# Meta-token states in two row groups, a written order of additions, and a residual added in PSUM, in a hybrid decoder layer

## The chip, the cores and the metric

The kernel runs on one core of one Trainium2 chip. The time is device microseconds of one execution; the number given is the median over several runs. A core has TensorE (PE in the profile; its weight loads are listed apart as PEld), VectorE (DVE), ScalarE (ACT), GpSimd (POOL) and SyncE (SP, which only issues transfers here). Products go into PSUM, which has eight banks of 512 fp32 columns; the other engines take them from there.

## The reference

One decoder layer on 512 tokens of width 1024, with 16 learned meta tokens put ahead of them (528 positions):

- `u = rmsnorm(h)`, and `proj = u @ w_in`, which is cut into the inputs of two branches and two sigmoid gates.
- The pooling branch takes causal means over windows of 2, 4, 8 and 16 positions, subtracts the input, and goes through a grouped matrix and `w_pool_up`.
- The state-space branch (SSD) has 8 groups of 4 heads with 64 channels. Tokens are worked on in chunks of 128; the 16 meta tokens are a chunk of their own, the first. Each chunk gives a state `sum over its tokens of B * (decay * dt * x)`, 128 x 64 for each head; states are carried on from chunk to chunk, `st[c+1] = decay_c * st[c] + (state of chunk c)`, and read out with C. So the meta chunk's product is `st[0]`: a contraction over only 16 positions, 128 x 256 for a group's four heads.
- `h = h + (gate_pool * y_pool + gate_ssd * y_ssd) @ w_o`, then `h = h + relu(rmsnorm(h) @ w_ff1)^2 @ w_ff2`, and a last rmsnorm with the weight `final_norm_w`. The 16 meta rows are dropped.

All is in fp32. Only the results of the 512 tokens are returned.

## The kernel before

**Precision.** Most products are made of halves: an fp32 number x is split into `hi`, x rounded to the type fp32r by a ScalarE copy, and `lo = x - hi`, by a VectorE subtraction. A product then takes three matmuls, hi x hi, hi x lo, lo x hi. A product of plain fp32 operands, as in the SSD part, is carried out as two passes, each with its own weight load and its own row in the trace.

**Stages.** Weights come in blocks of 128 x 1024 in a fixed order: SyncE's queue loads a block into one of three `raw` buffers (L85, L107), ScalarE writes `whi` (L93), VectorE `wlo` (L94), with four buffers of each. In order of time there are: the norm and the first projections; eight SSD groups, each woven by generators with the projections of the next group (`weave`); the `psp` products; the pooling stage with the `psl` products; the merge with `w_o`; the MLP in products over halves and sums of halves (Strassen's scheme in Winograd's form), and the last chunk of the MLP straight into the output.

**A group of the SSD** (`ssd`). TensorE transposes three chunks of B (`ptb`, L474) and B's 16 meta columns (L475), the meta columns of the two x tiles (`ptm`, L480), and the x tiles (`ptx`, L488). ScalarE takes B out (`btok`, `btm`, L476 and L477), VectorE multiplies x by dt (`xdtm`, L481; `xdt`, L489) and by the decay (`xddm`, L494; `xdd`, L495). Then come C x B (`pcb`, L522) and the states (`pst`): the meta product (L529), with 16 rows of `btm` as weights and 256 columns of `xddm`, and three products of full chunks (L531), two products to a bank. ScalarE copies `st[0]` out (L533), VectorE carries the states on (L538, L539), and `po` (L550) and `py` (L556) are the outputs. `dtm` and `decm` hold dt and decay of the meta positions, 16 partitions with all 32 heads beside each other; `dt_out` (L374 to L387) makes them by transposes and a small product.

**The `psl` stage.** The last two of the 16 rows of y are multiplied into `psl` (8 products, in four PSUM buffers), and each is added onto `acc[d]` by VectorE (L897). After it in the program come the blocks `wgb` and the last pool gate (`pgp`), the grouped matrix (`pg`), and `pool_pair`, which takes two raw blocks `a1` and `a2`, forms sums of their halves in `sm` (L818, L819) and splits them (`whiA`, `whiS`, `whiD`, `whiB`) for products with u.

**The end.** For each of four row tiles t and two column halves, products go into PSUM (L1491), VectorE adds them onto `ht`, which holds the residual (L1494), ScalarE sums the squares (L1368), VectorE multiplies by `fw` (L1498). `finish` makes the reciprocal root (L1376 to L1380) and scales the row tile on both engines (L1381, L1383). The last half of the last row tile is done in two parts of 256 columns.

**What sets the order.** Each engine works through a queue in a fixed order. That order isn't the program's: a planner fills it ahead of time from the program's order, the dependences and its own estimates of durations, and an instruction later in the program goes ahead where the earlier one would wait. `with tc.issue_after(i)` holds what is issued under it behind instruction i on the same engine. Before the change, L818 is held behind `psl_split`, the last subtraction of a weight split ahead of `wgb`.

Of the kernel before, what the change touches and what calls it, by code (L numbers as in the profile page):

```python
# [14 lines left out]
P = 128  # L15
D = 1024
SEQ = 512
NM = 16
# [45 lines left out]
def kernel(ctx: ExitStack, tc, xT, x, w, f1, f2, vec, fnw, out):  # L64
# [22 lines left out]
    def block_part(t, c):  # L87
        block_load(t, c)
        block_split(t, c)

    def block_split(t, c):
        b, raw, hi, lo = t
        act.copy(hi[:, c], raw[:, c])  # L93
        split_end[0] = dve.tensor_tensor(lo[:, c], raw[:, c], hi[:, c].bitcast(F32), op=ALU.subtract)  # L94

    split_end = [None]

    def block():
        t = block_tiles()
        block_part(t, slice(0, 1024))  # L100
        return t[2:]
# [52 lines left out]
    dtm = const.tile([NM, 2, HEADS], F32, name="dtm")  # L154
    dec = const.tile([P, 4, HEADS], F32, name="dec")
    cdec = const.tile([P, 4, HEADS], F32, name="cdec")
    decm = const.tile([NM, HEADS], F32, name="decm")
# [183 lines left out]

    v, e, s, s2, pl, dt, acs = (dtile(n) for n in ("dv", "de", "ds", "ds2", "dpl", "ddt", "dacs"))
# [27 lines left out]
    def dt_out():  # L370

        pt = psum1("pt_dt")
        for j, src in enumerate((dt, acs)):
            pe.transpose(pt[:, j * P : (j + 1) * P], src[:, :P], ident)  # L374
            pe.transpose(pt[:NM, 256 + j * H : 256 + (j + 1) * H], src[:H, P:], ident[:H, :H])
        dve.tensor_copy(dtok.rearrange("p a c h -> p (a c h)"), pt[:, :256])
        dve.tensor_copy(dtm.rearrange("p a h -> p (a h)"), pt[:NM, 256 : 256 + 2 * H])
# [3 lines left out]
        pe.matmul(pq[:NM, 128 : 128 + H], sel[:NM, 1, :NM], dtm[:, 1, :], start=True, stop=True)  # L381
        fl = lambda t: t.rearrange("p c h -> p (c h)")
        dve.tensor_tensor(fl(dec), pq[:, :128], fl(dtok[:, 1, :, :]), op=ALU.subtract)
        dve.tensor_tensor(decm, pq[:NM, 128 : 128 + H], dtm[:, 1, :], op=ALU.subtract)
# [73 lines left out]
    def ssd(g, cur):  # L458
# [10 lines left out]
        xdtm = gs.tile([NM, R, 64], F32, tag="xdtm", name=f"xdtm{g}")  # L469
        btok = gs.tile([P, 3, P], F32, tag="btok", name=f"btok{g}")  # L470
        btm = gs.tile([NM, P], F32, tag="btm", name=f"btm{g}")
# [3 lines left out]
        pe.transpose(ptb[:NM, 3 * P :], bt[:, :NM], ident)  # L475
        act.copy(btok.rearrange("p c n -> p (c n)"), ptb[:, : 3 * P])  # L476
        b_meta[g] = act.copy(btm, ptb[:NM, 3 * P :])  # L477
        pm = psum1(f"ptm{g}")
        for i in range(2):
            pe.transpose(pm[:NM, i * P : (i + 1) * P], xc[:, i, :NM], ident)  # L480
        dve.tensor_tensor(xdtm, pm[:NM, :256].rearrange("p (r d) -> p r d", r=R),  # L481
                          bc(dtm[:, 0, hs], 64), op=ALU.mult)
# [10 lines left out]
        xddm = gs.tile([NM, R, 64], F32, tag="xddm", name=f"xddm{g}")  # L493
        dve.tensor_tensor(xddm, xdtm, bc(decm[:, hs], 64), op=ALU.mult)  # L494
# [33 lines left out]
        pv = [pss[c // 2][:, (c % 2) * 256 : (c % 2) * 256 + 256] for c in range(4)]  # L528
        pe.matmul(pv[0], btm, flat(xddm), start=True, stop=True)  # L529
        for c in range(3):  # L530
# [1109 lines left out]
```

## Time and profile before

| | us |
|---|---|
| median of 3 runs | 1003.55 (1003.0 to 1003.87) |
| profiled execution, its own time | 1003.78 |
| its span in the trace | 1002.1 |
| TensorE busy | 993.4 |
| VectorE busy | 793.0 |
| ScalarE busy | 602.2 |
| GpSimd busy | 88.1 |

The granted TensorE clock was 0.998 in the profiled execution. A row of the trace in order of time begins with the start and the duration in us, then engine, line, operation, what is written and read, shapes and count; brackets at its end give how long the engine was idle ahead of it and what released it. Matmuls overlap their neighbours, so a sum of durations is more than the time that they take: the step from one start to the next is what counts. A row with x8 covers from the first start to the last end.

### The profile page before, as it was taken

How to read it: one execution, taken by the hardware profiler on the slowest of the kernel's cores; microseconds unless marked ns; L12 is line 12 of the kernel's file. 1: busy time of each engine (PE TensorE's matmuls, PEld its weight loads, DVE VectorE, ACT ScalarE, POOL GpSimd, SP SyncE). 2: the span in 40 equal slices, each digit the busy share in tenths (PEclk: the TensorE clock that was granted, in tenths of full speed). 3: DMA queues.
4: the chain of work that ended last, by engine and by line, in shares of the span. 5: the costliest groups of instructions: out<-in, count | busy, mean ns of one | idle time of the engine just before them, and what ended most of it. 6: DMA issues, size and time to landing. Idle time of an engine off the chain costs nothing.

```text
span 1002.1 us, 15532 instructions
## 1 busy us (share of the span) xinstructions
PE 993.4 (99%) x6093; PEld 877.8 (88%) x6093; DVE 793.0 (79%) x1147; ACT 602.2 (60%) x838; POOL 88.1 (9%) x148
## 2 busy tenths in 40 slices
PE   9999999999999999999999999999999999999997
PEld 7889898999889998988898888888889999999986
DVE  7988797979736687978789567877988888878885
ACT  8675958585827339483255343377666656656654
POOL 0022101111002011002210001121100000000000
PEclk9999999999999999999999999999999999999999
DMA  7278753677238635407987632779764454464432
GB/s 248 89 284 227 221 159 117 200 181 235 64 103 258 162 106 149 143 27 223 293 190 226 227 105 72 227 175 321 187 195 148 149 188 148 147 191 146 126 105 85
DMA packets 56202, 171.47 MB, mean 171 GB/s; under 512 B 6400, under 2 KB 7744, under 8 KB 55104
## 3 DMA queue, kind: packets, MB, share of 16 engines
q1 hardware_dynamic: 36576, 105.86, 32.4%
q0 software_dynamic: 18832, 63.71, 24.2%
q8 instruction: 48, 0.79, 0.3%
q10 hardware_dynamic: 720, 0.91, 0.3%
q14 instruction: 26, 0.21, 0.1%
HBM read 161.90 MB, written 48.40 MB: 210 GB/s over the span
## 4 chain that ended last, share of the span: by engine, by line
PE 97%; DMA 1%; DVE 1%; ACT 0%; issue 0%; SPq 0%; ACTq 0%; DVEq 0%
PE px L191 12%; PE px L1288 8%; PE alpha L1356 6%; PE pz L191 6%; PE px L193 6%; PE px L1291 4%; PE alpha L1359 3%; PE pgp L191 3%; PE pz L193 3%; PE pgs L191 3%; PE py L556 2%; PE pso L127 2%; PE po L550 2%; PE pso L128 1%; PE wo_alpha L1050 1%; PE pgp L193 1%
## 5 line engine op out<-in xcount | busy, mean ns | idle before, releaser
L93 ACT CAST whi<-raw 128x1024 fp32r<-128x1024 f32 (+2 forms) x98 | 98.6, 1015 | 105.3 <-PE px L193 30.9
L94 DVE TENSOR_TENSOR wlo<-raw,whi 128x1024 fp32r<-128x1024 f32 (+2 forms) x98 | 114.6, 1176 | 55.4 <-ACT whi L93 33.9
L191 PE MATMUL px<-uh,whi 128*128 128x264 f32 (+1 forms) x448 | 113.2, 291 | 0.0
L193 PE MATMUL px<-ul,whi 128*128 128x264 f32 (+1 forms) x448 | 110.5, 285 | 0.0
L191 PEld LDWEIGHTS px<-uh,whi 128*128 128x128 f32 x448 | 84.6, 189 | 1.8 <-issue 1.4
L193 PEld LDWEIGHTS px<-ul,whi 128*128 128x128 f32 x448 | 84.2, 188 | 0.4 <-issue 0.2
L1063 DVE TENSOR_TENSOR ht<-ht,alpha 128x1024 f32<-128x1024 f32 x35 | 42.7, 1219 | 29.5 <-PE alpha L1356 29.5
L986 ACT CAST shi<-rawf 128x1024 fp32r<-128x1024 f32 x42 | 44.2, 1052 | 28.8 <-PE alpha L1359 18.3
L191 PE MATMUL px<-uh,wlo 128*128 128x264 f32 (+1 forms) x448 | 58.5, 283 | 0.0
L191 PEld LDWEIGHTS px<-uh,wlo 128*128 128x128 f32 x448 | 55.9, 188 | 0.0
L1356 PE MATMUL alpha<-shi,hh 128*128 128x512 f32 x140 | 55.2, 394 | 0.0
L1359 PE MATMUL alpha<-shi,hl 128*128 128x512 f32 x140 | 54.7, 391 | 0.0
L987 DVE TENSOR_TENSOR slo<-rawf,shi 128x1024 fp32r<-128x1024 f32 x42 | 51.1, 1218 | 0.6 <-ACT shi L986 0.6
L1291 PE MATMUL px<-vsl,shi 128*128 128x256 f32 x192 | 47.4, 280 | 0.0
L1288 PE MATMUL px<-vsh,shi 128*128 128x256 f32 x192 | 47.4, 281 | 0.0
L193 PE MATMUL pz<-ul,whi 128*128 128x512 f32 x112 | 43.6, 389 | 0.0
L191 PE MATMUL pz<-uh,whi 128*128 128x512 f32 x112 | 43.6, 389 | 0.0
L577 DVE RECIPROCAL rs<-rs 128x128 f32<-128x128 f32 x32 | 27.2, 908 | 13.9 <-ACT rs L575 13.8
L1356 PE MATMUL alpha<-slo,hh 128*128 128x512 f32 x140 | 37.4, 389 | 0.0
L1288 PEld LDWEIGHTS px<-vsh,shi 128*128 128x128 f32 x192 | 36.2, 188 | 0.9
L1291 PEld LDWEIGHTS px<-vsl,shi 128*128 128x128 f32 x192 | 36.1, 188 | 0.9
L1291 PE MATMUL px<-vl,shi 128*128 128x256 f32 x144 | 36.1, 283 | 0.0
(550 smaller groups left out, 2857.0 us busy)
## 6 DMA issues: line engine op xcount, KB each, us to landing
raw<-in_w SPq DMA_DIRECT2D x104, 512.0 KB, 4.5
f_t<-in_f POOLq DMA_DIRECT2D x38, 512.0 KB, 6.8
f_s<-in_f POOLq DMA_DIRECT2D x26, 512.0 KB, 8.7
b<-in_f SPq DMA_DIRECT2D x21, 512.0 KB, 4.7
rawf<-in_f SPq DMA_DIRECT2D x36, 256.0 KB, 3.2
rawf<-f_t SPq DMA_DIRECT2D x36, 256.0 KB, 2.9
abc<-acs_d POOLq DMA_DIRECT2D x8, 1024.0 KB, 7.5
f_t<-f_t POOLq DMA_DIRECT2D x12, 512.0 KB, 4.3
```

Of the source, the lines that this page charges most:

```text
L93: act.copy(hi[:, c], raw[:, c])
L94: split_end[0] = dve.tensor_tensor(lo[:, c], raw[:, c], hi[:, c].bitcast(F32), op=ALU.subtract)
L191: pe.matmul(o, wt, rhs[0][k][:, c], start=part == 0 and k == 0, stop=part == 1 and k == NK - 1)
L193: pe.matmul(o, wt, rhs[1][k][:, c], start=False, stop=False)
L577: dve.reciprocal(rs[:, ctok(c)], rs[:, ctok(c)])
L986: splits.append((act.copy(hi, src), dve.tensor_tensor(lo, src, hi.bitcast(F32), op=ALU.subtract)))
L987: dve.tensor_tensor(lo, src, hi.bitcast(F32), op=ALU.subtract)))
L1063: added[0] = dve.tensor_tensor(o, o, src, op=op)
L1288: pe.matmul(ps, m, f[k][0], start=start and not low and k == 0, stop=stop and low == 1 and k == 3, skip_group_check=True)
L1291: pe.matmul(ps, m, f[k][1], start=False, stop=False, skip_group_check=True)
L1356: pe.matmul(ps[t], hh[:, p, seg, st], m, start=bool(first and not low and p == 0), stop=bool(last and low and p == 1), skip_group_check=True)
L1359: pe.matmul(ps[t], hl[:, p, seg, st], m, start=False, stop=False, skip_group_check=True)
```

## The change

Three parts.

**1. Two row groups.** The meta tiles get 48 partitions: heads 0 and 1 of a group in partitions 0 to 15, heads 2 and 3 in partitions 32 to 47. `dt_out` copies the 16 columns three times beside each other before it transposes them, and picks the heads of each row group. In `ssd`, ScalarE copies the meta columns of B, and of x, into a tile `meta` (three stretches of 16 columns each), from which one transpose of B's and one of x's meta columns are made, instead of one and two. The meta product becomes two products of 128 columns, one from each row group, each into its own bank; the product of the third chunk is cut into two halves of 128 columns likewise, and so are the copy of `st[0]` and the last addition of the states.

**2. The order of additions.** The subtraction of `wgb`'s split is held behind the third `psl` addition; L818 is held behind the first and L819 behind the second.

**3. The last residual.** For the last 256 columns of the last row tile, the residual is split into its halves (in `rq`, beside an identity matrix in fp32r), and two products with the identity put it into PSUM ahead of the other twelve. The addition onto `ht` goes, and the squares and the multiplication by `fw` read PSUM.

```
-    def block_split(t, c):
+    def block_split(t, c, behind=None):
         act.copy(hi[:, c], raw[:, c])
-        split_end[0] = dve.tensor_tensor(lo[:, c], raw[:, c], hi[:, c].bitcast(F32), op=ALU.subtract)
+        with tc.issue_after(behind.ins) if behind is not None else nullcontext():
+            dve.tensor_tensor(lo[:, c], raw[:, c], hi[:, c].bitcast(F32), op=ALU.subtract)
...
+    M2 = 32 + NM
+    ROWS = (slice(0, NM), slice(32, M2))
+    dtm = const.tile([M2, 2, HEADS], F32, name="dtm")[:, :, : HEADS // 2]
+    decm = const.tile([M2, HEADS], F32, name="decm")[:, : HEADS // 2]
+    dve.memset(dtm, 0.0)
+    dve.memset(decm, 0.0)
...
         for j, src in enumerate((dt, acs)):
             pe.transpose(pt[:, j * P : (j + 1) * P], src[:, :P], ident)
-            pe.transpose(pt[:NM, 256 + j * H : 256 + (j + 1) * H], src[:H, P:], ident[:H, :H])
+            thrice = dp.tile([H, 3, NM], F32, name=f"thrice{j}")
+            dve.tensor_copy(thrice, src[:H, P:].unsqueeze(1).to_broadcast([H, 3, NM]))
+            pe.transpose(pt[:M2, 256 + j * H : 256 + (j + 1) * H], thrice.rearrange("p a t -> p (a t)"), ident[:H, :H])
-        dve.tensor_copy(dtm.rearrange("p a h -> p (a h)"), pt[:NM, 256 : 256 + 2 * H])
+        dve.tensor_copy(acm, pt[:NM, 256 + H : 256 + 2 * H])
+        for a, rows in enumerate(ROWS):
+            dve.tensor_copy(by(dtm[rows]), of(pt[rows, 256 : 256 + 2 * H], a))
...
+        act.copy(meta[:, 1, :M2].rearrange("p (a t) -> p a t", a=3), bt[:, :NM].unsqueeze(1).to_broadcast([P, 3, NM]))
+        act.copy(meta[:, 0, :M2].rearrange("p (a t) -> p a t", a=3), xq[:, :3, :NM])
...
-        pe.transpose(ptb[:NM, 3 * P :], bt[:, :NM], ident)
+        pe.transpose(ptb[:M2, 3 * P :], meta[:, 1, :M2], ident)
...
-        for i in range(2):
-            pe.transpose(pm[:NM, i * P : (i + 1) * P], xc[:, i, :NM], ident)
+        pe.transpose(pm[:M2, :P], meta[:, 0, :M2], ident)
...
-        pe.matmul(pv[0], btm, flat(xddm), start=True, stop=True)
-        for c in range(3):
-            pe.matmul(pv[c + 1], btok[:, c, :], xdd[:, c, :, :].rearrange("p r d -> p (r d)"),
-                      start=True, stop=True)
-        y_first[g] = st0 = act.copy(flat(st[0]), pv[0])
+        half = (slice(0, 2), slice(2, R))
+        for b, rows in enumerate(ROWS):
+            pe.matmul(pss[b][:, :P], btm[rows], flat(xddm[rows]), start=True, stop=True)
+        for c in range(2):
+            pe.matmul(pss[c][:, P : 3 * P], btok[:, c, :], flat(xdd[:, c, :, :]), start=True, stop=True)
+        for b in range(2):
+            pe.matmul(pss[b][:, 3 * P :], btok[:, 2, :], flat(xdd[:, 2, half[b], :]), start=True, stop=True)
+        for b in range(2):
+            y_first[g] = st0 = act.copy(flat(st[0][:, half[b], :]), pss[b][:, :P])
...
-        dve.tensor_tensor(acc[d], acc[d], ps, op=ALU.add)
-    psl_split = split_end[0]
-    wgb = block()
+        psl_add.append(dve.tensor_tensor(acc[d], acc[d], ps, op=ALU.add))
+    wgb = block(psl_add[2])
...
-    nxt = pool_pair(POOL_ORDER[1], psl_split)
+    nxt = pool_pair(POOL_ORDER[1], psl_add[:2])
...
+    rq = qp.tile([P, 1024], F32R, tag="quarter", name="rq")
+    end = slice(768, 1024)
+    act.copy(rq[:, :P], ident)
+    act.copy(rq[:, 256:512], ht[:, 3, end])
+    dve.tensor_tensor(rq[:, 512:768], ht[:, 3, end], rq[:, 256:512].bitcast(F32), op=ALU.subtract)
...
+                if a:
+                    for n2 in range(2):
+                        pe.matmul(ps, rq[:, :P], rq[:, 256 * (n2 + 1) : 256 * (n2 + 2)], start=n2 == 0, stop=False,
+                                  skip_group_check=True)
...
-                dve.tensor_tensor(ht[:, t, cs], ht[:, t, cs], ps, op=ADD)
-                squares(t, cs, n)
+                src = ps
+                if not a:
+                    src = ht[:, t, cs]
+                    dve.tensor_tensor(src, src, ps, op=ADD)
+                squares(t, cs, n, src)
...
-                dve.tensor_tensor(outs[t][:, cs], ht[:, t, cs], fw[:, cs], op=ALU.mult)
+                dve.tensor_tensor(outs[t][:, cs], src, fw[:, cs], op=ALU.mult)
```

More of the change, by code (lines that the diff above doesn't have):

```diff
@@ L380, in dt_out @@
                   start=True, stop=True)
-        pe.matmul(pq[:NM, 128 : 128 + H], sel[:NM, 1, :NM], dtm[:, 1, :], start=True, stop=True)
+        pe.matmul(pq[:M2, 128 : 128 + H], sel[:NM, 1, :M2], acm, start=True, stop=True)
         fl = lambda t: t.rearrange("p c h -> p (c h)")
         dve.tensor_tensor(fl(dec), pq[:, :128], fl(dtok[:, 1, :, :]), op=ALU.subtract)
-        dve.tensor_tensor(decm, pq[:NM, 128 : 128 + H], dtm[:, 1, :], op=ALU.subtract)
+        for a, rows in enumerate(ROWS):
+            dve.tensor_tensor(by(decm[rows].unsqueeze(1)), of(pq[rows, 128 : 128 + H], a), by(dtm[rows, 1:2, :]),
+                              op=ALU.subtract)
         act.activation(fl(dec), fl(dec), AF.Exp)
@@ L474, in ssd @@
             pe.transpose(ptb[:, c * P : (c + 1) * P], bt[:, tok(c)], ident)
[L475 removed]
+        pe.transpose(ptb[:M2, 3 * P :], meta[:, 1, :M2], ident)
         act.copy(btok.rearrange("p c n -> p (c n)"), ptb[:, : 3 * P])
[L477 removed]
+        b_meta[g] = act.copy(btm, ptb[:M2, 3 * P :])
         pm = psum1(f"ptm{g}")
[L479 to L482 removed]
+        pe.transpose(pm[:M2, :P], meta[:, 0, :M2], ident)
+        h2 = slice(2 * g, 2 * g + 2)
+        dve.tensor_tensor(xdtm, pm[:M2, :P].rearrange("p (r d) -> p r d", r=2),
+                          bc(dtm[:, 0, h2], 64), op=ALU.mult)
         for b in range(2):
@@ L538, in ssd @@
             dve.tensor_tensor(st[c + 1], st[c], bc(cdec[:, c, hs], 64), op=ALU.mult)
-            dve.tensor_tensor(flat(st[c + 1]), flat(st[c + 1]), pv[c + 1], op=ALU.add)
+            for o, p in ([(st[c + 1], pss[c][:, P : 3 * P])] if c < 2
+                         else [(st[3][:, half[b], :], pss[b][:, 3 * P :]) for b in range(2)]):
+                dve.tensor_tensor(flat(o), flat(o), p, op=ALU.add)
         for rs_ in ((slice(0, 2), slice(2, R)) if g == G - 1 else (slice(0, R),)):
@@ L816, in pool_pair @@
         fa = split_form(a1, both, f"A{p}")
-        with tc.issue_after(behind.ins) if behind is not None else nullcontext():
+        behind = behind or (None, None)
+        with tc.issue_after(behind[0].ins) if behind[0] is not None else nullcontext():
             dve.tensor_tensor(sm[:, h1], a2[:, h1], a2[:, h2], op=ALU.add)
-        dve.tensor_tensor(sm[:, h2], sm[:, h1], a1[:, h1], op=ALU.subtract)
+        with tc.issue_after(behind[1].ins) if behind[1] is not None else nullcontext():
+            dve.tensor_tensor(sm[:, h2], sm[:, h1], a1[:, h1], op=ALU.subtract)
         fs = split_form(sm, both, f"S{p}")
@@ L893 @@
     un = units()
+    psl_add = []
     for d in range(NK):
@@ L1364, with squares @@
     q5v = [psum1(f"q5_{t}") for t in range(2)]
-    def squares(t, c, n):
+    def squares(t, c, n, src):
         j = m1p.tile([P, SEQ], F32, tag=f"m1_{t}", name=f"sq{t}_{n}")
-        act.activation(j[:, : c.stop - c.start], ht[:, t, c], AF.Square, accum_out=fs[:, t, n : n + 1])
+        act.activation(j[:, : c.stop - c.start], src, AF.Square, accum_out=fs[:, t, n : n + 1])
     outs = {}
@@ L1487 @@
                         x0 = p * 512 + a
-                        f = i == 0 and not (T == 0 and half == 0)
+                        f = i == 0 and not (T == 0 and half == 0) and not a
                         i += 1
```

22 lines of the change are left out of this document (12 added, 10 removed).

## The prediction

> **What bounds the kernel now.** I read the page's engine shares and the chain of waits first, then the waits of TensorE, then its instructions in order of time in the three places that the change touches.
>
> ```profile
> span 1002.1 us, 15532 instructions
> ...
> PE 993.4 (99%) x6093; PEld 877.8 (88%) x6093; DVE 793.0 (79%) x1147; ACT 602.2 (60%) x838; POOL 88.1 (9%) x148
> ...
> PE 97%; DMA 1%; DVE 1%; ACT 0%; issue 0%; SPq 0%; ACTq 0%; DVEq 0%
> ```
>
> TensorE is busy 99% of the span and is 97% of the chain that ended last. So a product taken away there is worth its own issue time, as long as nothing else becomes late; work added on VectorE or ScalarE is free until TensorE waits for it. TensorE's own waits are few; the one inside the program that counts is this, in the stage of the `psl` products:
>
> ```profile
> PE psl L127 <- DVE acc L897: 0.5, 1, 0.5
> ```
>
> **Part 1, the meta rows of a group (eight times).** TensorE in group 0, in order of time:
>
> ```profile
> 69.00 0.27 PE L475 MATMUL ptb<-ident,bt 128*16 128x128 f32 x1
> 69.11 0.38 PE L480 MATMUL ptm<-ident,xc 128*16 128x128 f32 x2
> 69.33 1.04 PE L488 MATMUL ptx<-ident,xc 128*128 128x128 f32 x8
> ...
> 76.02 1.05 PE L522 MATMUL pcb<-ct,bt 128*128 128x128 f32 x8
> 77.01 0.69 PE L529 MATMUL pst<-xddm,btm 16*128 16x256 f32 x2
> 77.63 1.56 PE L531 MATMUL pst<-xdd,btok 128*128 128x256 f32 x6
> 78.84 0.47 PE L191 MATMUL px<-uh,whi 128*128 128x258 f32 x1
> ```
>
> Two transposes of meta rows take 69.11 to 69.33, 0.11 us each. One of the two goes in each group: 8 x 0.11 = **-0.88 us**. The remaining ones have 48 weight columns instead of 16, but stream the same 128 columns of the identity, as L488 with 128 weight columns does at 1.04 us for eight, so I cost them at no change.
>
> A 128-column fp32 pass steps by (1.05 - 0.275) / 7 = 0.11 us (L522: first start to last end, less one pass's 0.275). A 256-column pass is two of these, 0.22. The meta product has two passes of 256 columns and holds TensorE from 77.01 to 77.63, 0.62 us: 0.44 of streaming and 0.18 of going in and out of the 16-row form. After the change there are two products of 128 columns, in partitions 0 to 15 and 32 to 47, two passes each. No row here shows two row groups at work together. Bounds: if they don't overlap, four passes of 0.11 stream for the same 0.44, gain 0; if they overlap fully, two steps of 0.11, 0.22, gain 0.22. The nearest row is the products of 64 output columns, two column groups of the array:
>
> ```profile
> 446.88 1.09 PE L556 MATMUL py<-abc,xdt 128*64 128x128 f32 x16
> 447.90 1.34 PE L550 MATMUL po<-ct,st 128*128 128x128 f32 x8
> ```
>
> Sixteen passes end within 1.09 us where eight full-width ones take 1.05 (L522): the column groups run in pairs. I take full overlap for the row groups: 8 x 0.22 = **-1.76 us** (bounds 0 and -1.8). The third chunk's product (128 x 256) is cut in two halves of 128 columns so that each lands in its own bank: four passes of 0.11 for two of 0.22, at most **+0.1 us** over all groups.
>
> Beside this, ScalarE gets two copies more per group (three stretches of 16 columns into `meta`) and one more of `st[0]`; by the row below a copy of 128 columns is 0.25 us. VectorE's meta multiplications halve in width and one addition becomes two, about even.
>
> ```profile
> L477 ACT COPY btm<-ptb x8: 247/249/251, 72.1 to 437.5; 16x128 f32<-16x128 f32 x8
> ...
> 429.13 0.65 ACT L408 ACTIVATE xc<-xc 128x528 f32<-128x528 f32 x1
> 429.80 1.28 ACT L501 ACT_TABLE_LOAD   x1
> ...
> 432.18 0.70 ACT L506 ACTIVATE abc<-abc,dtok 128x128 f32<-128x128 f32 x2
> ...
> 434.18 1.02 ACT L451 ACTIVATE zt<-pz 128x1024 f32<-128x1024 f32 x1
> ...
> 433.81 0.27 PE L475 MATMUL ptb<-ident,bt 128*16 128x128 f32 x1
> ```
>
> This adds a wait: TensorE's meta transposes now stand behind ScalarE's two copies, and behind them on TensorE all of the next group's projections. In group 7 the inputs are ready at 429.13 + 0.65 = 429.78, and the transposes start at 433.81: 4.0 us of cover for 0.5 us of copies. ScalarE already issues later lines of the same group (L501, L506) ahead of `zt` (L451), so the copies should stand ahead of it too. I cost the wait at nothing; without that cover it is the slow rival below.
>
> `dt_out` gets two copies ahead of its transposes and three more small VectorE operations. At 0.20 us each by the row below, 0 to 0.4 us can show on TensorE for the two that it waits for; I take **+0.1**. The two memsets at the start fall into the first load of x, which ends at 6.28 (2.19 + 4.09); nothing.
>
> ```profile
> 52.51 0.20 DVE L377 COPY dtm<-pt_dt 16x64 f32<-16x64 f32 x1
> ...
> 2.19 4.09 DMA xt<-in_xT
> ```
>
> **Part 2, the order of additions.** TensorE, then VectorE, then the chain, around the eight `psl` products:
>
> ```profile
> 487.64 0.39 PE L127 MATMUL psl<-yh,whi 128*128 128x512 f32 x1
> ...
> 489.00 0.39 PE L127 MATMUL psl<-yh,whi 128*128 128x512 f32 x1
> ...
> 493.71 0.47 PE L127 MATMUL psl<-yh,whi 128*128 128x512 f32 x1 [0.47 <-DVE acc L897]
> ...
> 499.27 0.39 PE L191 MATMUL pgp<-uh,whi 128*128 128x512 f32 x1
> ...
> 510.32 0.28 PE L841 MATMUL pxx<-t42h,whiS 128*128 128x260 f32 x1
> ...
> 482.06 1.23 DVE L94 TENSOR_TENSOR wlo<-raw,whi 128x1024 fp32r<-128x1024 f32 x1 [4.07 <-ACT whi L93]
> ...
> 489.19 0.69 DVE L818 TENSOR_TENSOR sm<-raw 128x512 f32<-128x512 f32 x1 [2.36 <-DMA raw<-in_w]
> 489.92 0.69 DVE L819 TENSOR_TENSOR sm<-sm,raw 128x512 f32<-128x512 f32 x1
> ...
> 491.13 1.22 DVE L94 TENSOR_TENSOR wlo<-raw,whi 128x1024 fp32r<-128x1024 f32 x1
> ...
> 492.88 0.68 DVE L897 TENSOR_TENSOR acc<-acc,psl 128x512 f32<-128x512 f32 x1
> ...
> 483.32 5.75 DMA raw<-in_w
> ```
>
> One `psl` takes 489.00 - 487.64 = 1.36; eight take 10.88, but 499.27 - 487.64 = 11.63 went by: 0.75 lost. The first addition waits behind L818, which stood idle 2.36 us for a load, and with four banks the fifth product waits for it. With the first addition ahead of L818 this loss goes: **-0.75 us** (bounds 0 and -0.75).
>
> What it costs: the split of `wgb` (482.06) now stands behind the third addition. That product ends about 487.64 + 3 x 1.36 = 491.7, so addition and split end at 491.7 + 0.7 + 1.2 = 493.6. Its raw buffer is the one that `a2` is loaded into, so that load, issued at 483.32 now, moves to 493.6 and lands 5.75 later, 499.4. SyncE's next load stands behind it. L818 and L819 (0.7 each), ScalarE's cast and VectorE's split (1.05 and 1.2) end at 503.0; TensorE wants them at 510.32 less the gain. Six us of cover: nothing.
>
> **Part 3, the end.** VectorE and ScalarE after the last product:
>
> ```profile
> 995.15 0.28 PE L1491 MATMUL last<-slo,hh 128*128 128x256 f32 x1
> 995.27 0.28 PE L1491 MATMUL last<-shi,hl 128*128 128x256 f32 x1
> ...
> 995.59 0.42 DVE L1494 TENSOR_TENSOR ht<-ht,last 128x256 f32<-128x256 f32 x1
> ...
> 996.10 0.42 ACT L1368 ACTIVATE sq<-ht 128x256 f32<-128x256 f32 x1 [0.93 <-DVE ht L1494]
> ...
> 996.97 0.16 DVE L1380 RECIPROCAL rt<-rt 128x1 f32<-128x1 f32 x1 [0.50 <-ACT rt L1378]
> ...
> 972.77 1.05 ACT L986 CAST shi<-w__9582 128x1024 fp32r<-128x1024 f32 x1 [1.67 <-PE alpha L1359]
> ...
> 973.68 1.22 DVE L1063 TENSOR_TENSOR ht<-ht,alpha 128x1024 f32<-128x1024 f32 x1 [0.81 <-PE alpha L1356]
> ```
>
> Two products of 256 columns come in, each a step of 0.12: the last one ends at 995.55 + 0.24 = 995.79. The squares then start about 0.04 later (as L1494 did after 995.55), at 995.83 instead of 996.10: **-0.27 us**, all of which reaches the reciprocal at 996.97. The two copies and the subtraction that make the halves (some 0.6 and 0.4 us) fit the idle 1.67 us of ScalarE and 0.81 of VectorE; without that cover the last split is late by 0.4.
>
> The multiplication by `fw` now reads the same bank as the squares; before, both read SBUF. The Trainium skill, "PSUM — Partial Sum Buffer", section "PSUM bank collisions raise a hardware error", has two engines' reads of one bank kept apart. By that rule the multiplication starts only at 996.25 and ends near 996.7, just where the reciprocal wants VectorE, and the part gives -0.23 instead of -0.27. No row here shows two engines on one bank.
>
> **Sum:** -0.88 - 1.76 + 0.1 + 0.1 - 0.75 - 0.27 = -3.46. The profiled execution took 1003.78 (span 1002.1), so 1000.3; the median shown is 0.23 lower, so **1000.1**.
>
> **The rivals.**
> *Row groups don't overlap:* no row shows them doing so; against it stand the column groups. The 1.76 falls away: 1001.9.
> *Strict order:* the passes start in the order written, so the second group's first pass waits for the first group's second. Three steps of 0.11 in place of four: 0.11 a group, 0.9 in all, 1001.0. The `py` row speaks against it, since pairs could not form. The Trainium skill, "TensorE: Matmul & The Clock Gate", Part 3, says that matmuls start and end in strict order; by that rule this rival holds.
> *The late `a2` load eats part 2:* if VectorE's queue has L818 ahead of the fourth addition, the eighth product waits for 499.4 + 1.4 + 0.7 = 501.5 in place of 497.2: +4.3, and the gain of 0.75 turns. More likely only later additions stand behind it, and the 0.75 alone is lost with some 0.5 us beside: 1001.3.
> *Slower:* the copies stand behind `zt` on ScalarE. In group 7 the transposes then wait until 434.18 + 1.02 + 0.5 = 435.7 instead of 433.81: +1.9. If it happens in all seven groups that have a `zt` ahead of them, 7 x 1.9 = 13.3: 1013. It decides from two groups on (3.8 against 3.46). Against it: L501 and L506 stand ahead of `zt`.
>
> **How the numbers follow.** Forecast 0.53 (its own range 999.2 to 1001.2); no overlap 0.14; strict order 0.11; late load 0.13; copies behind `zt` 0.09. No change means within 0.2%, about what this measurement can tell: 1001.5 to 1005.6. Faster takes 0.50 of the forecast, 0.08 of strict order and 0.06 of the two at 1001.3 and 1001.9: 0.64. Slower is most of the last rival, 0.07, and 0.01 of the late load: 0.08. The rest is 0.28. The range of 999.0 to 1003.4 holds the first four with their bounds and leaves out the last.
>
> **What would show it.** L529 in the changed trace: four products per group whose starts come in pairs, and about 0.4 us from the first to L531. One `ptm` transpose, with no wait of TensorE for ScalarE's `meta`. `psl` from first start to `pgp` in 10.9 us, and no wait for L897. The last squares 0.28 us after the last product's end, with no addition between. I would be wrong if TensorE waits for `meta`, if `psl` still takes over 11.5, or if new waits appear in the groups because the planner orders them anew.

## The result, and the profile after

| us | median | lowest to highest |
|---|---|---|
| before, on the same chip | 1003.71 | 1003.0 to 1004.88 |
| after | 1009.32 | 1008.23 to 1012.97 |

The changed kernel is slower: 1.0056 times the time before, 95% interval 1.0043 to 1.0068. 1000.1 had been predicted, with a range up to 1003.4. The profiled execution took 1009.17 us, its span is 1007.4 (before 1002.1).

The page of the changed kernel, with the span, the engine shares and the chain that ended last:

```profile
span 1007.4 us, 15618 instructions
...
PE 993.5 (99%) x6119; PEld 879.0 (87%) x6119; DVE 793.6 (79%) x1162; ACT 604.6 (60%) x863; POOL 88.4 (9%) x148
...
PE 89%; ACT 7%; DVE 2%; issue 1%; DMA 0%; SPq 0%; ACTq 0%; DVEq 0%
```

TensorE has as much busy time as before, but now 7% of the chain lies on ScalarE, where it had been 0%. What TensorE waited for in the changed kernel, with the total, the number of times and the longest in us:

```profile
PE ptb L495 <- ACT meta L488: 1.9, 1, 1.9
...
PE po L576 <- DVE st L565: 1.0, 1, 1.0
PE pxx L869 <- DVE pu L883: 0.9, 1, 0.9
PE py L582 <- issue: 0.7, 1, 0.7
PE pxx L869 <- ACT pu L875: 0.4, 1, 0.4
...
```

None of these stood in the list of before. The one of before in the `psl` stage is gone.

**What went as worked out.** TensorE in group 0, in order of time:

```profile
79.23 0.49 PE L551 MATMUL pst<-xddm,btm 16*128 16x128 f32 x4
79.65 1.13 PE L553 MATMUL pst<-xdd,btok 128*128 128x256 f32 x4
80.62 0.61 PE L555 MATMUL pst<-xdd,btok 128*128 128x128 f32 x4
80.98 0.37 PE L197 MATMUL px<-uh,whi 128*128 128x258 f32 x1
81.19 0.28 PE L199 MATMUL px<-ul,whi 128*128 128x258 f32 x1
...
79.23 0.30 PEld L551 LDWEIGHTS pst<-xddm,btm 16*128 16x128 f32 x4
```

The meta block goes from 79.23 to 79.65: 0.42 us, and before it was 0.62. Four weight loads of 0.18 us each lie within 0.30 us, so they run in pairs. So do the passes: in the trace, two start at 79.23 and two at 79.44 to 79.45, two steps of 0.21. The full chunks take 80.98 - 79.65 = 1.33, 0.12 more than before (1.21), as the third chunk is cut; 0.1 of that comes back in the next step (81.19 - 80.98 = 0.21, before 0.31). In all 0.18 us a group.

The `psl` stage starts at 491.77 and its successor `pgp` at 502.65: 10.88 us in place of 11.63. VectorE there:

```profile
493.96 0.68 DVE L926 TENSOR_TENSOR acc<-acc,psl 128x512 f32<-128x512 f32 x1
...
498.17 1.22 DVE L95 TENSOR_TENSOR wlo<-raw,whi 128x1024 fp32r<-128x1024 f32 x1
...
503.45 1.22 DVE L114 TENSOR_TENSOR wloA<-raw,whiA 128x1024 fp32r<-128x1024 f32 x1
506.87 0.69 DVE L845 TENSOR_TENSOR sm<-raw 128x512 f32<-128x512 f32 x1 [2.19 <-DMA raw<-in_w]
```

The additions go through, but the split of `wgb` stands at 498.17, behind the fourth of them, and `sm` waits for `a2`. At the end there is no addition between the last product and the squares:

```profile
1001.11 0.28 PE L1530 MATMUL last<-shi,hl 128*128 128x256 f32 x1
1001.49 0.38 ACT L1397 ACTIVATE sq<-last 128x256 f32<-128x256 f32 x1 [0.70 <-PE last L1530]
...
1001.99 0.42 DVE L1540 TENSOR_TENSOR out<-last,fw 128x256 f32<-128x256 f32 x1 [0.76 <-ACT sq L1397]
1002.34 0.15 DVE L1409 RECIPROCAL rt<-rt 128x1 f32<-128x1 f32 x1
```

The first `last` product starts 5.61 us later than before and the reciprocal 5.37 (1002.34 against 996.97): 0.24 gained, 0.27 predicted.

**Where it was lost.** TensorE in group 0, and then ScalarE in the same stretch:

```profile
70.50 0.29 PE L199 MATMUL px<-ul,whi 128*128 128x264 f32 x1
72.74 0.29 PE L495 MATMUL ptb<-ident,meta 128*48 128x128 f32 x1 [1.95 <-ACT meta L488]
```

```profile
70.89 1.04 ACT L93 CAST whi<-raw 128x1024 fp32r<-128x1024 f32 x1 [5.45 <-PE px L199]
71.84 0.72 ACT L631 ACTIVATE m<-m,vs 128x512 f32<-128x512 f32 x1
72.47 0.21 ACT L488 COPY meta<-bt 128x48 f32<-128x48 f32 x1
72.59 0.23 ACT L489 COPY meta<-xc 128x48 f32<-128x48 f32 x1
```

ScalarE stands idle for 5.45 us in front of a cast; behind the cast stand a sigmoid of the first gates and then the copies. Their inputs have been there since the projections of group 0. TensorE waits 1.95 us.

### The profile page after: what moved, and what is told of

The parts are those of the page before. It is cut to its first block, busy times and chain, and to the rows that moved or that the text cites. A ratio compares the mean times of both kernels' runs of the same rounds, so it can differ in the third digit from the quotient of the medians.

```text
span 1007.4 us, 15618 instructions
## 1 busy us (share of the span) xinstructions
PE 993.5 (99%) x6119; PEld 879.0 (87%) x6119; DVE 793.6 (79%) x1162; ACT 604.6 (60%) x863; POOL 88.4 (9%) x148
## 4 chain that ended last, share of the span: by engine, by line
PE 89%; ACT 7%; DVE 2%; issue 1%; DMA 0%; SPq 0%; ACTq 0%; DVEq 0%
PE px L197 11%; PE px L1317 8%; PE alpha L1385 6%; PE px L199 5%; PE px L1320 4%; PE pz L197 4%; PE alpha L1388 3%; PE pgs L197 3%; PE pgp L197 3%; PE pz L199 2%; PE py L582 2%; PE pgp L199 1%; PE pf L128 1%; PE pf L127 1%; PE pf L130 1%; PE pgs L199 1%
```

## Where the time went, stage by stage

Start of a product less its start in the kernel before, both counted from group 0's first transpose, in us (from the starts in the two traces, one profiled execution each; runs are named by the sections below):

| | C x B, group 0 | z, group 3 | psp, last | pgp after psl | gate after the pooled pairs | last |
|---|---|---|---|---|---|---|
| after | +2.07 | +3.88 | +3.99 | +3.23 | +5.02 | +5.46 |
| r_after (the same kernel) | +3.90 | +5.66 | +5.78 | +5.02 | +5.02 | +5.25 |
| e3_rows | +2.20 | +3.71 | +3.90 | +3.64 | +3.64 | +4.03 |
| e2_adds | 0 | 0 | +0.59 | -0.16 | -0.16 | -0.19 |
| e5_wgb | +2.20 | +3.64 | +3.73 | +2.97 | +2.97 | +3.58 |
| e4_meta_place | -0.09 | +1.05 | +1.72 | +0.96 | +0.96 | +1.91 |
| e12_place_free | -0.10 | +1.62 | +2.24 | +1.48 | +1.48 | +1.44 |
| e6_twice | -0.10 | +1.56 | +1.98 | +1.22 | +1.22 | +1.72 |
| e7_shift | 0 | +0.16 | +0.68 | -0.08 | +1.58 | +2.00 |
| e7b_free | 0 | +0.16 | +0.74 | -0.03 | -0.03 | +0.58 |
| e11_some | +0.01 | +0.79 | +0.94 | +0.18 | +0.19 | +0.13 |
| e13_rows_dve | 0 | -0.50 | -0.28 | -1.03 | -1.03 | -0.92 |
| e10_adds_tail | 0 | -0.01 | +0.73 | -0.02 | -0.02 | -0.02 |
| s1_cut1 | 0 | -0.15 | -0.45 | -1.20 | +0.47 | +0.71 |
| s3_act | 0 | +1.64 | +3.45 | +2.70 | +2.70 | +3.02 |
| s4_dve | 0 | -0.01 | +0.09 | -0.67 | -0.67 | -0.60 |
| s2_cut4 | 0 | -2.22 | +6.68 | +5.92 | +5.93 | +6.91 |
| e14_btm_dve | 0 | +0.54 | +2.76 | +2.01 | +2.00 | +2.00 |
| e1_tail | 0 | 0 | -0.05 | -0.09 | -0.09 | -0.02 |

How far such a number can be read: e2_adds, e10_adds_tail and s4_dve have the same instructions as the kernel before up to `psp` (s4_dve one more a group on VectorE), TensorE takes them in the same order in the groups, and they differ there by +0.59, +0.73 and +0.09. Below 0.7 at `psp` nothing is concluded. Between the gate and `last`, after loses another 0.44, and several runs 0.2 to 1.0; no run here explains that.

## The three parts, each alone

e1_tail has only part 3, e2_adds only part 2, e3_rows only part 1 of the diff.

> The kernel before with the end part alone: the residual of the last 256 columns goes into PSUM by two products of its halves, and the last addition falls away. Theory (each part keeps its price on its own engine, all losses come from new waits in the groups and in the pooled products): the time from the last product's end to the end of the program shrinks by about 0.5 us, the two added products cost 0.25, so the end comes 0.3 us earlier, 1003.4; TensorE's starts up to the last product agree with the kernel before within 0.2. Rival (the end part does part of the damage, through the two copies and the subtraction ahead of the last splits): starts in the last stage late by 0.3 us or more, time 1003.8 or above.

Measured: 1003.90, 0.9996 times before (0.9986 to 1.0005). Starts up to `last` agree within 0.1; the span less the start of `last` is 0.3 shorter. The part gives what was worked out, too little for the median to show.

> The kernel before with the order of additions alone. Theory (the order gains its 0.75 us in the psl stage, and the late load of a2 takes it back in the first pooled products): starts equal up to psl, 0.75 earlier at the gate after psl, about 1.0 later than before at the first product after the three pooled pairs, with waits of 0.5 to 1.0 us of pxx for pu; about 1004.7 in all. Rival (the waits in the pooled products come from the 3.4 us by which the row groups had shifted everything, which moves loads and engines against each other): no such waits here, gain of 0.75 kept to the end, about 1002.9.

Measured: 1003.52, 0.9996 (0.9987 to 1.0005). `psl` gains 0.75 and nothing comes after it: alone, the late load of `a2` costs nothing. That was the rival's case.

> The kernel before with the row groups alone. Theory (the products gain what was priced, -0.21 us a group and -0.11 for the transpose, and the wait for the meta copies in group 0, the wait for the state additions in group 3 and smaller ones cost more): a meta block of 0.42 us instead of 0.62 in all groups, +2.1 us by the pcb products of group 0, +4 by the psp products, and then no further growth: end +4.0, about 1007.7. Rival (the waits in the groups come from the other two parts' change of the order): gain of 2.5 us at psp, 1001.2.

Measured: 1007.96, 1.0045 (1.003 to 1.0059). The wait in group 0 is there:

```profile
PE ptb L495 <- ACT meta L488: 2.1, 1, 2.1
```

So part 1 alone makes the loss, 3.9 of it by the end of the groups, 2.2 of these in group 0.

## Group 0: the place of one tile

`meta` comes from the pool `gs`, which opens when the first stage's pools close and takes their memory. e4_meta_place gives it memory of its own:

```
-        meta = gs.tile([P, 2, 64], F32, tag="meta", name=f"meta{g}")
+        meta = gc.tile([P, 2, 64], F32, tag="meta", name=f"meta{g}", bufs=1)
```

> The changed kernel with meta in the pool of the group inputs, in memory of its own, instead of the pool whose memory the first stage's tiles (the scale of x among them) held. Theory (in group 0 the copies into meta are put late on ScalarE because their place is still in use by the first stage; nothing else is the matter with them): the copies run over 5 us earlier, ahead of the sigmoids of the first gates, TensorE's transposes wait for nothing, and the changed kernel gets 2.1 us faster, about 1007.2; the other losses stay. Rival (the copies wait for ScalarE's own queue: casts and sigmoids stand ahead whatever the place): the wait of 1.9 us stays and the time too, 1009.3.

Measured: 1004.69, 1.0007 (0.9998 to 1.0016). The copies of group 0 start at 37.8 and 46.6 us, ahead of the first gates, and TensorE runs through:

```profile
L488 ACT COPY meta<-bt x8: 217/225/232, 37.8 to 407.7; 128x48 f32<-128x48 f32 x8
...
68.77 0.49 PE L494 MATMUL ptb<-ident,bt 128*128 128x128 f32 x3
69.09 0.27 PE L495 MATMUL ptb<-ident,meta 128*48 128x128 f32 x1
```

The mechanism is shown: the place alone moved the copies, and the wait went. But the gain was larger than the 2.1 expected. r_after, the changed kernel itself once more, tells a part of why.

> The changed kernel itself once more, beside the next one on the same chip. Theory (wait of 2.1 us in group 0 and the later ones are there in every execution, the pooled ones in part of them): 5 us over the kernel before, 1009. Rival (a good part of the difference was one chip's or one execution's): 1006 or less.

Measured: 1007.76, 1.0035 (1.0022 to 1.0047). Its profiled execution, 1009.14, lost 3.9 us in group 0, not 2.07, and nothing in the pooled pairs. TensorE in group 0 of r_after, and then windows of it, in which the number behind POOL's is the granted TensorE clock:

```profile
70.71 0.29 PE L199 MATMUL px<-ul,whi 128*128 128x264 f32 x1
73.22 0.29 PE L495 MATMUL ptb<-ident,meta 128*48 128x128 f32 x1 [2.23 <-ACT meta L488]
...
74.87 0.42 PE L199 MATMUL px<-ul,whi 128*128 128x264 f32 x1
75.09 0.42 PE L197 MATMUL px<-uh,whi 128*128 128x264 f32 x1
```

```profile
68.00:70.60 2.60, 2.60 (x20) 2.35 (x19) 0.69 (x1) 0.00 (x0) 0.00 (x0) 1.00 1.00 410
74.30:77.30 3.00, 3.00 (x16) 3.00 (x15) 2.95 (x7) 2.96 (x3) 1.10 (x3) 0.50 0.97 274
78.20:79.20 1.00, 1.00 (x11) 1.00 (x10) 0.00 (x0) 1.00 (x5) 0.30 (x1) 1.00 1.07 213
```

From 74.3 to 77.3 the clock is at half, and a pass steps by 0.22 us in place of 0.12. The wait itself is 73.22 - 70.71 less a step of 0.12, 2.4 us; the other 3.9 - 2.4 = 1.5 are the slow passes. So the wait has a second price in some executions. In after (1.95 us idle), e3_rows and e5_wgb (2.1) the clock stayed at 1.0; here the idle time was 2.23. The executions that weren't profiled point the same way: e3_rows took 1007.3 to 1008.0 at a mean granted clock of 0.998 to 0.999, and 1009.8 and 1010.1 at 0.997. No trace shows where in those two the clock fell.

## The pooled pairs: a late load ahead of `pu` in VectorE's queue

e5_wgb lets `wgb`'s split go where the planner puts it, and is otherwise the changed kernel:

```
-    wgb = block(psl_add[2])
+    wgb = block()
```

> The changed kernel with the split of wgb not held behind the third addition (the sums still stand behind the first two additions). Theory (the 1.8 us of waits in the first pooled products come from two things together: the held split makes the load of a2 late, and the wait in group 0 makes it later still, so that it stands behind 512 KB loads of GpSimd's sums): the load of a2 is issued some 12 us earlier, as before, the waits of pxx for pu go, the 0.75 us of psl stays; end 1.8 us earlier, about 1007.5. Rival (the waits come from the row groups' shift alone, whatever the split): pxx still waits about 1.6 us, 1009.3.

Measured: 1009.20, 1.0043 (1.003 to 1.0057). In the profiled execution, 1007.34, the waits of `pxx` are gone and the 0.75 is kept; it was the fastest, and the median doesn't show the 1.8. The other three took 1009.0 to 1009.6, at a mean granted clock of 0.997 to 0.998 where the profiled one had 0.999; that would fit the second price of the wait in group 0, but no trace shows it.

How the 1.8 us came about is told by VectorE's queue, and by the product that waited:

```profile
517.34 0.69 DVE L845 TENSOR_TENSOR sm<-raw 128x512 f32<-128x512 f32 x1 [2.55 <-DMA raw<-in_w]
517.95 0.42 DVE L877 TENSOR_TENSOR pu<-pu,py 128x260 f32<-128x260 f32 x1
...
520.63 0.42 DVE L883 TENSOR_TENSOR pu<-pu,pxx 128x260 f32<-128x260 f32 x1
...
521.10 0.39 PE L869 MATMUL pxx<-t42h,whiB 128*128 128x260 f32 x1 [0.88 <-DVE pu L883]
```

The sum of the next pair stands ahead of `pu` in VectorE's queue. It waits 2.55 us for a load that was issued at 512.05, and that load took an ordinary 5.2; it was issued late, since its raw buffer came free late, behind the sums and splits that had waited for `a2` until 506.87. So a late `a2` reaches TensorE a load further on, by way of `pu`. In e4_meta_place, which holds the split too, `sm` starts at 502.26 without a wait, and nothing is lost.

Why `a2` was late in the changed kernel: the transfers that GpSimd issued there, in order of time (e2_adds and e4_meta_place hold the split too, and have no wait):

```profile
498.62 0.84 POOL L741 DMA_DIRECT2D f_t<-in_f  x1 [6.65 <-DMA f_t<-in_f]
499.91 0.82 POOL L742 DMA_DIRECT2D f_s<-in_f  x1 [0.45 <-DMA f_s<-in_f]
```

`a2` was issued at 499.46, between two of GpSimd's 512 KB transfers, and landed at 506.8: 7.3 us. In e4_meta_place it was issued at 497.13, ahead of GpSimd's (498.30), and landed at 500.9: 3.7 us; in e2_adds it took 5.0. e7_shift and e7b_free (below) differ in the hold alone: with it, the profiled execution loses 1.66 in the pooled pairs, without it nothing. But s1_cut1 has no hold either and loses 1.67, at the load after: VectorE there,

```profile
512.41 0.69 DVE L819 TENSOR_TENSOR sm<-raw 128x512 f32<-128x512 f32 x1 [4.61 <-DMA raw<-in_w]
```

was waiting for a load issued at 504.93, with a transfer of GpSimd at 505.10. It took 7.4 us; in e10_adds_tail, where GpSimd's went out 1.35 us ahead of SyncE's, 4.8. So a load that took 2.6 or 3.6 us longer than in the run beside it goes with 1.7 or 1.8 us lost on TensorE. That a GpSimd transfer beside it makes a load slow isn't shown: between 485 and 522 us, loads of SyncE with a GpSimd transfer issued within a microsecond took over 6.8 us 17 times, but 3.4 to 4.6 us 13 times (in e6_twice `a2` went out 0.16 us behind one and took 3.5); without one, 9 of 56 took over 6. The hold isn't the only cause: of six profiled kernels with it two lose time there (after, e7_shift; r_after, e2_adds, e4_meta_place and e6_twice don't), of those without it s1_cut1 alone.

e12_place_free has both edits, `meta` from `gc` and `block()`:

> The changed kernel with meta in memory of its own and the split of wgb not held behind the third addition. Theory (place of meta costs 2.1 us in group 0 and some 0.7 us in group 2, and with the early load of a2 no pooled wait can come): 4 to 5 us under the changed kernel, about 1004.5, and no run 1.5 us over the others. Rival (the place has no part in it, what the earlier run with meta in its own memory gained was the pooled waits alone): 1007 or more.

Measured: 1004.68, 1.0004 (0.9996 to 1.0013), beside r_after on one chip: the place of `meta` and the hold together cost 3.1 us of median. By the medians the place has all of it: against the kernel before on their own chips, e4_meta_place, with the hold, is at 1.0007, e12_place_free at 1.0004, and e5_wgb, with the old place and no hold, at 1.0043.

## The groups: what TensorE saves is given back

With `meta` in its own memory, the groups still end 1.7 to 2.2 us late, though TensorE has 8 x (0.18 + 0.11) = 2.3 us less to do. First a doubling of the copies into `meta`, in e6_twice:

```
         act.copy(meta[:, 1, :M2]...)
         act.copy(meta[:, 0, :M2]...)
+        act.copy(meta[:, 1, :M2]...)
+        act.copy(meta[:, 0, :M2]...)
```

> The changed kernel with meta in memory of its own, and each of the two copies into meta done twice (the second a repeat): 0.45 us more of ScalarE in each group and nothing else. Theory (what is still lost with meta in its own memory, waits of py in group 1, of po in group 2 and of psp behind group 7, comes from ScalarE's and VectorE's queues, which are full in groups 1 to 3, so that each added 0.1 us there goes on to TensorE): these waits grow by 0.3 to 0.5 us each and the starts behind group 3 are another 0.7 to 1.5 us late against the run with the copies done once; about 1005.8. Rival (the waits come from the products' new shape and order, and the copies lie beside other work): the same starts within 0.3 us, 1004.7.

Measured: 1005.64, 1.0018 (1.0006 to 1.0031). Unclear: at the last `psp` the profiled execution stands at +1.98, between the +1.72 of e4_meta_place and the +2.24 of e12_place_free, but the median is 1.0 above that of e4_meta_place, as the theory has it. What the copies' own time costs stays open.

e7_shift has row groups and no `meta`: the three transposes stay, and the second row group is written by shifted copies.

```
-        b_meta[g] = act.copy(btm, ptb[:NM, 3 * P :])
+        for rows in ROWS:
+            b_meta[g] = act.copy(btm[rows], ptb[:NM, 3 * P :])
...
+        for b, rows in enumerate(ROWS):
+            h2 = slice(R * g + 2 * b, R * g + 2 * b + 2)
+            dve.tensor_tensor(xddm[rows], xdtm[:, 2 * b : 2 * b + 2], bc(decm[:, h2], 64), op=ALU.mult)
```

> The row groups without meta: the transposes as in the kernel before (16 rows, three of them, nothing ahead of them), the second copy of btm's 16 rows written by ScalarE to partitions 32 to 47, and VectorE's decayed xddm written in two products to rows 0 to 15 and 32 to 47; with the order of additions and the end part as in the changed kernel. Theory (row groups gain 0.18 us a group on TensorE, the losses come from copies that stand ahead of TensorE's transposes and from full queues): no wait in group 0, 8 x 0.18 = 1.5 gained by psp less waits of at most 1 us, then 0.75 at psl and 0.3 at the end: 1.5 to 2.5 us under the kernel before, about 1002.2. Rival (shifted writes or the split products cost as much as meta did): 1004.5 or more.

> The same as e7_shift, with the split of wgb not held behind the third addition. Theory (the hold gains nothing by itself, since the sums' place behind the first additions is what frees the psl products): psl takes 10.9 us and pxx doesn't wait, the same time as e7_shift within 0.3 us. Rival (the hold is what lets the additions through, as the split stands ahead of them otherwise): psl loses 0.4 us or more, 1002.7 or above.

Measured: e7_shift 1004.08, 1.0004 (0.9995 to 1.0013); e7b_free 1003.89, 1.0000 (0.9991 to 1.0009). No wait in group 0, `psl` at 10.9 in both (so the hold is needed for nothing), but nothing gained at `psp`: +0.74 where the same kernel without row groups, e10_adds_tail, has +0.73.

e10_adds_tail is the kernel before with parts 2 and 3 of the change, `block()` without its argument:

> The kernel before with the order of additions (sums behind the first two additions, wgb's split not held) and the end part, without the row groups. Theory (these two parts keep their price when nothing else moves): 0.75 earlier behind psl, 0.3 at the end, about 1.0 us under the kernel before, 1003.1, no pooled wait. Rival (the additions' gain needs the held split): 1003.8.

Measured: 1003.48, 0.9990 (0.9981 to 0.9999): parts 2 and 3 without the hold are faster than the kernel before.

e11_some has the row groups of e7b_free under a condition, and else the code of before:

```
+        rg = g in (0, 1, 5, 6)
```

> As e7b_free, with the row groups only in groups 0, 1, 5 and 6, where the run with all eight showed TensorE ahead at the group's end; groups 2, 3, 4 and 7 as in the kernel before. Theory (each group's gain is its own, the losses sit in the groups where the state additions come just in time): 4 x 0.18 = 0.7 us more than the order of additions and the end part give alone, about 1002.4. Rival (whatever a group gains is given back at the next place where VectorE or ScalarE come just in time): 1003.1 or more.

Measured: 1004.22, 0.9998 (0.9989 to 1.0007). Picking groups doesn't help; the rival holds.

Four kernels then put single doses on e10_adds_tail: two and eight passes of TensorE fewer in groups 1 to 7, added copies on ScalarE, an added product on VectorE.

```
-                    if part == 0:
+                    if part == 0 and k < NK - cut:     (1 and 4, for the projection of C alone)
                         pe.matmul(o, wt, rhs[1][k][:, c], start=False, stop=False)
...
         b_meta[g] = act.copy(btm, ptb[:NM, 3 * P :])
+        b_meta[g] = act.copy(btm, ptb[:NM, 3 * P :])     (twice more, s3_act)
...
         dve.tensor_tensor(xddm, xdtm, bc(decm[:, hs], 64), op=ALU.mult)
+        dve.tensor_tensor(xddm, xdtm, bc(decm[:, hs], 64), op=ALU.mult)     (s4_dve)
```

> The order of additions and the end part alone (e10_adds_tail), and in groups 1 to 7 two passes of TensorE fewer: the projection of C leaves out the product of the last eighth of u's low half with the high weights. That takes 2 x 0.12 = 0.24 us a group from TensorE and nothing from any other engine; what is computed differs from the reference by that small term. Theory (in the groups TensorE's gain is given back because VectorE and ScalarE come just in time there): less than half of the 7 x 0.24 = 1.7 us arrives at the last psp product, 1002.7 or above. Rival (the gain of the row groups was lost by what the row groups add, not by the place): 1.5 us arrive, 1001.8.

> The same with eight passes fewer in each of groups 1 to 7 (the last half of u's low half is left out of the projection of C): 0.96 us a group, 6.7 in all. Theory: a part only arrives at the last psp product, 2 to 4 us, as TensorE then waits for VectorE and ScalarE in most groups; 1000 to 1001.5. Rival: over 6 us arrive, 997.

> The order of additions and the end part alone, with ScalarE's copy of btm done three times in each group: 0.3 us more of ScalarE a group, nothing ahead of TensorE's transposes, TensorE's and VectorE's work as it is. Theory: ScalarE comes just in time in the groups, so some of the 8 x 0.3 = 2.4 us reaches TensorE: 0.5 to 1.5 us later at the last psp product, 1004 to 1005. Rival (VectorE alone is the one that comes just in time): within 0.3 us, 1003.5.

> The order of additions and the end part alone, with VectorE's product for xddm done twice in each group: 0.33 us more of VectorE a group, nothing else. Theory: VectorE comes just in time in the groups, 0.5 to 1.5 us later at the last psp product, 1004 to 1005. Rival (ScalarE alone is the one that comes just in time): within 0.3 us, 1003.5.

Measured: s1_cut1 1002.93, 0.9987 (0.9977 to 0.9996); s2_cut4 1008.65, 1.0045 (1.003 to 1.006); s3_act 1005.90, 1.0016 (1.0007 to 1.0026); s4_dve 1003.47, 0.9994 (0.9985 to 1.0003). At the last `psp`, against e10_adds_tail: s1_cut1 -1.2 of the 1.7 taken away, more than the half that the theory allowed; s3_act +2.7 for the 8 x 0.3 = 2.4 put in; s4_dve -0.6 for 2.6 put in. The work added on VectorE doesn't arrive, within what can be read. For ScalarE the dose isn't a clean one. The pages of e10_adds_tail and of s3_act:

```profile
PE 994.0 (99%) x6095; PEld 878.1 (88%) x6095; DVE 792.9 (79%) x1147; ACT 603.1 (60%) x840; POOL 88.3 (9%) x148
PE 995.4 (99%) x6095; PEld 878.4 (87%) x6095; DVE 793.2 (79%) x1147; ACT 602.4 (60%) x853; POOL 88.4 (9%) x148
```

With 16 copies more, ScalarE has only 13 instructions more and isn't busier: the planner wrote its queue anew, with three ACT_TABLE_LOAD fewer, and TensorE's order in the groups is another too, where s4_dve kept that of e10_adds_tail. So a change of ScalarE's queue cost 2.7 us here; whether by the copies' time or by the new order, s3_act can't tell. What TensorE waited for in s3_act:

```profile
PE pz L191 <- DVE xc L406: 0.5, 2, 0.3
PE psp L680 <- ACT yh L586: 0.5, 1, 0.5
```

s2_cut4 went against both theories: ahead by 2.2 at group 3, then ten us lost in group 4, where TensorE waits for ScalarE and the clock falls. Its longest wait there, and its window from 248 to 268:

```profile
261.84 1.12 PE L488 MATMUL ptx<-ident,xc 128*128 128x128 f32 x4 [3.29 <-ACT rs L575]
...
248.00:268.00 20.00, 15.61 (x64) 12.17 (x62) 7.06 (x14) 14.34 (x17) 1.07 (x2) 0.83 0.29 100
```

Here ScalarE is what TensorE waits for as well; why its order is so much worse is open.

The last two move copies from ScalarE to VectorE. e13_rows_dve is e7b_free with the two added copies on VectorE:

```
-        for rows in ROWS:
-            b_meta[g] = act.copy(btm[rows], ptb[:NM, 3 * P :])
+        b_meta[g] = act.copy(btm[ROWS[0]], ptb[:NM, 3 * P :])
+        dve.tensor_copy(btm[ROWS[1]], ptb[:NM, 3 * P :])
...
+        y_first[g] = st0 = act.copy(flat(st[0][:, half[0], :]), pss[0][:, :P])
+        dve.tensor_copy(flat(st[0][:, half[1], :]), pss[1][:, :P])
```

> As e7b_free (row groups in all eight groups, three transposes as before, no meta), with the two copies that the row groups add, btm's second one and that of the second half of st[0], on VectorE instead of ScalarE. Theory (ScalarE is what comes just in time in groups 2, 3 and 7: s3_act gave it 0.3 us more a group and 2.4 us arrived at the end, while 0.33 more on VectorE cost nothing): with ScalarE's work as before, the 8 x 0.18 = 1.5 us of the row groups arrive, 1 to 1.5 us under the order of additions and the end part alone, about 1002.2. Rival (what TensorE gains is given back whatever the engine of the copies): 1003.4 or more.

e14_btm_dve is e10_adds_tail with

```
-        b_meta[g] = act.copy(btm, ptb[:NM, 3 * P :])
+        b_meta[g] = dve.tensor_copy(btm, ptb[:NM, 3 * P :])
```

> The order of additions and the end part alone (e10_adds_tail), with the copy of btm moved from ScalarE to VectorE: 0.16 us less of ScalarE's queue in each group, 0.2 more of VectorE's, TensorE's work as it is. Theory (ScalarE comes just in time, but TensorE had waits of less than 0.2 us there in the kernel before, so nothing is left to gain without TensorE's work getting less): within 0.3 us of e10_adds_tail, 1003.4. Rival (ScalarE holds TensorE up in the kernel before too): 0.5 to 1.3 us less, 1002.5.

Measured: e13_rows_dve 1003.06, 0.9993 (0.9983 to 1.0002), beside 1004.07 before; e14_btm_dve 1006.18, 1.0021 (1.0012 to 1.003). In e13_rows_dve a part of the row groups' gain arrives: -0.28 at the last `psp`, 1.0 under e7b_free and e10_adds_tail, of the 1.5 that the row groups take from TensorE. The edit against e7b_free is the engine of two copies; the planner's order changed with it, and 1.0 is little above the 0.7 below which nothing is concluded. One wait of the groups is left, in group 7:

```profile
PE po L561 <- DVE st L550: 0.6, 1, 0.6
```

Of the kernels that leave nothing out it has the lowest median against its own runs of before (-1.0 us; e10_adds_tail -0.7), but the interval takes in no change. e14_btm_dve is a miss, 2.1 us above before where no change was expected: TensorE is within 0.6 us of e10_adds_tail up to group 7, and then loses about 2 us there:

```profile
PE py L556 <- PE psp L678: 0.9, 1, 0.9
PE pst L529 <- DVE btm L477: 0.3, 1, 0.3
```

With `btm` on VectorE, TensorE waits for it, and the order of its own queue behind that is another. A copy off ScalarE is not a gain where the other engine delivers later.

## Why the prediction was wrong

- **The step that failed:** "This adds a wait ... I cost the wait at nothing". It rests on group 7, where the inputs lie ready 4.0 us before the transposes. In group 0 the copies stood behind a cast and a sigmoid, since the tile's memory was still in use by the first stage, and TensorE waited 1.95 us. The trace of before held the warning: ScalarE stands idle there ahead of the same cast,

```profile
70.14 1.05 ACT L93 CAST whi<-raw 128x1024 fp32r<-128x1024 f32 x1 [5.13 <-DMA raw<-in_w]
71.10 0.71 ACT L605 ACTIVATE m<-m,vs 128x512 f32<-128x512 f32 x1
71.72 0.46 ACT L476 COPY btok<-ptb 128x384 f32<-128x384 f32 x1
```

  and takes B out at 71.72, 2.4 us after TensorE had made it. Before, nobody on TensorE waited for that queue. The slow rival, copies behind `zt`, was right in kind (copies late on ScalarE), wrong in place and condition: group 0 has no `zt` ahead of it.
- **"Work added on VectorE or ScalarE is free until TensorE waits for it"**, and the copies "beside this": wrong for ScalarE in the groups. Copies of 0.3 us a group there cost 2.7 (s3_act, with the new order that came with them); VectorE, the busier of the two, took 0.33 a group for nothing (s4_dve). A window of the kernel before over group 2, busy us of PE, PEld, DVE and ACT behind its length:

```profile
150.10:198.90 48.80, 48.80 (x346) 44.57 (x345) 42.42 (x68) 35.21 (x47) 5.56 (x11) 1.00 0.50 157
```

  By it VectorE had 6.4 us free and ScalarE 13.6, so the share doesn't tell where added work shows. It is the part of the loss that after makes between group 0 and the last `psp`: 3.99 - 2.07 = 1.9 us, with 2 us of TensorE's saving gone beside it. How much of it is the copies' time, and how much the planner's other order, is open.
- **"Six us of cover: nothing"** for the late `a2`: the cover was reckoned for `whiS` and `wloS` alone, and they were in time. What it left out is the load after, whose raw buffer came free late, with `pu` behind its sum in VectorE's queue. Two sizes were off as well: with TensorE 4.1 us behind before at `psl`, the split should have ended at 497.7 and ended at 499.4, and the load was put at 5.75 and took 7.3. The profiled execution lost 1.8 us by it, r_after's nothing. The rival of the late load had the price (0.75 and 0.5) too low and the place wrong: the pooled products, not `psl`.
- **Row groups, -1.76 with +0.1:** the mechanism was right, pairs and a block of 0.42 for 0.62. The term is 8 x 0.18 = 1.5 on TensorE. The rival of strict order is refuted: three steps of 0.11 and the 0.18 would make a block of 0.51, and it took 0.42, with passes that start two by two. The Trainium skill, "TensorE: Matmul & The Clock Gate", Part 3, says that matmuls start and end in strict order; the trace doesn't tell which product a pass belongs to, so it shows only that this rival doesn't follow here, not that the rule fails.
- **Transposes, -0.88; `dt_out`, +0.1; `psl`, -0.75; end, -0.27:** measured 0.11 a group, +0.15 ahead of group 0 (e1_tail, which changes nothing there, has +0.60, so this can't be read), -0.75, -0.24. The multiplication by `fw` does start only after the squares (1001.99, released by ScalarE's `sq`). This agrees with the rule of the Trainium skill that the prediction named, "PSUM — Partial Sum Buffer", section "PSUM bank collisions raise a hardware error". The reciprocal follows the multiplication without idle time, where before it had waited 0.50 us for ScalarE's root.
- **What the text named as proof against it** came: TensorE waits for `meta`, and new waits stand in the groups.

## What to carry to other kernels

When an edit puts work of engine A ahead of engine B's critical instruction, look up A's queue at every instance of it, the first one above all: what A was idle for there, what stands ahead, and whose memory the new tile gets. Busy shares don't say which engine has room; a dose of added work on one engine can, if the orders of the other queues stayed as they were, so compare them first. A saving on the bounding engine can be given back by what the edit adds on another: here nothing of the row groups' 1.5 us could be read with the copies on ScalarE, and 1.0 with two of them on VectorE, in one profiled execution each.

## What was not expected of the hardware

- A wait of 2.23 us halved TensorE's clock for about 3 us (0.50, rows above), which cost another 1.5; waits of 1.95 and 2.1 didn't in the profiled executions. The Trainium skill, "TensorE: Matmul & The Clock Gate", Part 1, gives the idle window as about 3.4 us and calls it free-running; here two thirds of that were enough once.
- Less work on the bounding engine made the kernel slower: eight passes fewer a group, 6.7 us of TensorE, and 4.6 us more in the median (s2_cut4). The reason stays open.
- SyncE's 512 KB loads between 485 and 522 us took from 3.4 to 9.5 us in these runs, and a GpSimd transfer issued within a microsecond doesn't tell which (17 slow loads and 13 fast ones had one).
